# A chunk state summed in PSUM, and a square moved to ScalarE, in a hybrid RWKV-7 / RG-LRU / attention kernel

## The chip, the cores and the metric

The kernel runs on one core of a Trainium2 chip. The metric is the device time of one execution in microseconds. A core has five engines, each with its own in-order queue: TensorE (PE, with weight loads shown as PEld), VectorE (DVE), ScalarE (ACT), GpSimd (POOL) and SyncE (SP), which here issues the DMAs. SBUF is the working memory; PSUM is where TensorE writes its results, and VectorE and ScalarE read and write it too.

## The reference

Two layers over 512 tokens of width 1024. Each layer normalizes, projects to one wide vector, and runs three mixers side by side on slices of it: an RWKV-7 recurrence (8 heads of 64x64 state), an RG-LRU recurrence over 512 channels, and latent attention. Cut to what the change touches:

```python
def step(S, inp):                                  # RWKV-7, one token
    r_t, w_t, k_t, v_t, kk_t, b_t = inp
    sa = jnp.einsum('bhij,bhj->bhi', S, kk_t)
    S = S * w_t[:, :, None, :] - sa[..., None] * b_t[:, :, None, :] + v_t[..., None] * k_t[:, :, None, :]
    return S, jnp.einsum('bhij,bhj->bhi', S, r_t)
...
log_a = -LRU_C * gate_r * jax.nn.softplus(-lam)    # RG-LRU
a = jnp.exp(log_a)
bx = jnp.sqrt(-jnp.expm1(2.0 * log_a)) * (gate_i * xc)
_, h = lax.associative_scan(combine, (a, bx), axis=1)      # h_t = a_t h_(t-1) + bx_t
```

## The kernel before

All products with large weights are done as three float32r matmuls (L233, L234, L235): each operand is split into a rounded high part (ScalarE, L141) and the rest (GpSimd or VectorE, L229 and L211), and high x high, low x high and high x low are summed in PSUM. These projection matmuls are the bulk of TensorE's work, and the program threads them between the small matmuls of the recurrences.

The RWKV-7 recurrence runs in eight chunks of 64 tokens. `chunk(ch)` (L841) does one. If it is not the first, eight pairs of 64x64 matmuls with the state S (L849) correct the values, and two VectorE additions write them to UV (L852). Eight pairs with UV (L859) give the chunk's contribution `so`, in PSUM. The new state is (so + S) x pc, with pc the decay at the chunk's end, one number for each column: L863 adds, L864 multiplies; the first chunk has only a product (L866). The next chunk's L849 needs that state. Every second chunk also makes the outputs of the pair: matmuls with S (L877) and with UV (L883) into two PSUM tiles, a VectorE copy (L885) and a ScalarE square (L886) of each, and a reduction (L887). The small products of the chunks use `ck()`, which hands out two PSUM banks in turn.

The RG-LRU runs on four groups of 128 channels, in two pairs: `lru_b(0, 1)` and `lru_b(2, 3)`. For each group ScalarE makes a = exp(...) (helper line L138, after a table load, L136); GpSimd squares it (L702); VectorE makes (a^2 + 1) x th (L704) and a lower bound (L705); after another table load ScalarE takes the root (L138); GpSimd multiplies it into bx (L710); VectorE scans (L712; its opcode prints as SCALAR_TENSOR_TENSOR in the lists below); ScalarE squares the result (L716, L718), GpSimd sums the squares (L719), and VectorE applies gain and gate (L720). The convolution in front of the gates is three VectorE instructions (L681), and the gate matmuls behind it are L687. L691 is a GpSimd product of that part.

The order of this work comes from strings of step names. The stage of the change is the head of this one (H is `chunk`, B is `lru_b`, A the front half of the RG-LRU, f and t steps of projections):

```python
ORD3 = "B0 H0 H1 A2 H2 H3 A3 H4 H5 H6 H7 B1 N0 g0 g1 t0 t6 t1 ..."
```

Within that, a list scheduler orders the instructions of each engine by its own costs, so that an edited instruction can move its neighbours. Weights come through rings of buffers: three raw tiles (wr), four high (wH) and four low parts (wL).

Of the kernel before, what the change touches and what calls it, by code (L numbers as in the profile page):

```python
# [11 lines left out]
AF = mybir.ActivationFunctionType  # L12
ALU = mybir.AluOpType
# [34 lines left out]
def body(ctx, tc, x, wc, wl, wo, w2a2, gagx, wuq, wukv, vec, ln_g, fin_g, cst, out, depth=DEPTH):  # L48
    nc = tc.nc
    V, A, G = nc.vector, nc.scalar, nc.gpsimd  # L50
# [21 lines left out]
    def g2(shape=(128, 512)):  # L72
        return tl("g2", shape, F32, bufs=11)
# [59 lines left out]
    def act(out, in_, func, **kw):  # L133
        st = {AF.Sigmoid: "S", AF.Tanh: "S", AF.Sqrt: "Q"}.get(func, "E")
        if cur[0] != st:
            chained(A.preload_act_table_set(SETS[st]))  # L136
            cur[0] = st
        chained(A.activation(out=out, in_=in_, func=func, **kw))  # L138
# [182 lines left out]
    def one_layer(l):  # L321
# [375 lines left out]
        def lru_b(*js):  # L697
            for j in js:
                a, bx, th = st[j]
                act(a, a, AF.Exp, scale=nsp8[:, l, j:j + 1])  # L700
                a2 = g2()
                G.tensor_tensor(out=a2, in0=a, in1=a, op=ALU.mult)  # L702

                V.scalar_tensor_tensor(out=a2, in0=a2, scalar=1.0, in1=th, op0=ALU.add, op1=ALU.mult)  # L704
                V.tensor_scalar(out=a2, in0=a2, scalar1=1.0e-34, scalar2=None, op0=ALU.max)  # L705
                st[j] += (a2,)
            for j in js:
                a, bx, th, a2 = st[j]
# [130 lines left out]
        S = [None] * 8  # L839

        def chunk(ch):  # L841
# [11 lines left out]
            if ch < 7:  # L853
                so = ck([128, 4, 64])
                for p in range(4):
                    for e in range(2):
                        hr = slice(64 * e, 64 * e + 64)
                        hc = slice(e * 64, (e + 1) * 64)
                        PE.matmul(so[hr, p, :], BT[p][:, ch, hc], UV[:, p, ch, hc], start=True, stop=True)  # L859
                sn = S[ch + 1] = tl("S", [128, 4, 64], bufs=3)  # L860
                pc = PC[:, :, ch:ch + 1].to_broadcast([128, 4, 64])
                if ch:
                    V.tensor_tensor(out=sn, in0=so, in1=S[ch], op=ALU.add)  # L863
                    V.tensor_tensor(out=sn, in0=sn, in1=pc, op=ALU.mult)  # L864
                else:
                    V.tensor_tensor(out=sn, in0=so, in1=pc, op=ALU.mult)  # L866
            if par == 0:
                return
            yt = c2([128, 4, 2, 64])
# [357 lines left out]
```

## Time and profile before

| | us |
|---|---|
| three runs | 848.09, 848.45, 851.1 |
| median | 848.45 |
| profiled execution | 847.71 |
| its span | 845.9 |
| TensorE busy | 791.7 (94%) |
| VectorE busy | 538.9 (64%) |
| ScalarE busy | 519.3 (61%) |
| GpSimd busy | 353.3 (42%) |

The profile is of one execution. A row of the timeline gives the start in us from the span's start, the duration, the engine, the line, the operation with output and inputs by name, the count where neighbours are merged, and in brackets how long the engine stood idle before it and which engine's instruction ended that. A row that groups instructions gives their summed and mean durations, or in another view the least, median and greatest in ns. The windows give each engine's busy time in a stretch and the granted TensorE clock, where 1.00 is full rate. Durations of neighbours on one engine overlap a little, since the next one starts while the last one drains. A matmul's end is modelled.

### The profile page before, as it was taken

The numbers are of one execution on the slowest core, as the hardware profiler recorded it, in microseconds if no ns is written. First come the engines' busy times: TensorE is split into PE (matmuls) and PEld (weight loads), VectorE is DVE, ScalarE is ACT, GpSimd is POOL, SyncE is SP. The second block draws the span as 40 slices with busy tenths as digits, with TensorE's granted clock in tenths as the row PEclk, the third lists the DMA queues.
The fourth block names the chain that finished last, engine by engine and source line by source line (L and its number), as shares of the span: only waits on it lengthen the run. The fifth ranks groups of instructions, "written<-read, shape, count | busy, mean of one in ns | idle before, by whom it ended". The sixth has DMA issues, their size and how long they took to land. (4 is left out here: it accounts for less than half of the span.)

```text
span 845.9 us, 15219 instructions
## 1 busy us (share of the span) xinstructions
PE 791.7 (94%) x5696; PEld 619.4 (73%) x5696; DVE 538.9 (64%) x1115; ACT 519.3 (61%) x1018; POOL 353.3 (42%) x321
## 2 busy tenths in 40 slices
PE   4999999999879999999989999999998799999995
PEld 3878888886659877657778788888765697775674
DVE  5678776924977364774474966695367953577636
ACT  5667875657563576664467687845666436765635
POOL 0455557522452455022344556574143425530323
PEclk9999999999998999999999999999999899999998
DMA  7222134311113375123732233332001234731354
GB/s 246 98 76 74 66 111 132 112 58 33 33 39 113 120 229 193 55 90 92 272 122 89 75 100 100 101 112 92 30 26 43 80 95 140 244 120 50 112 174 162
DMA packets 49754, 91.07 MB, mean 108 GB/s; under 512 B 5520, under 2 KB 8336, under 8 KB 49680
## 3 DMA queue, kind: packets, MB, share of 16 engines
q1 hardware_dynamic: 49104, 89.05, 32.8%
q8 instruction: 45, 0.74, 0.4%
q10 hardware_dynamic: 576, 1.05, 0.3%
q14 instruction: 29, 0.24, 0.1%
HBM read 73.30 MB, written 16.78 MB: 106 GB/s over the span
## 5 line engine op out<-in xcount | busy, mean ns | idle before, releaser
L229 POOL TENSOR_TENSOR wL<-wr,wH 128x512 fp32r<-128x512 f32 (+1 forms) x148 | 196.8, 1336 | 283.9 <-ACT wH L141 270.4
L141 ACT ACTIVATE wH<-wr 128x512 fp32r<-128x512 f32 (+1 forms) x192 | 118.8, 622 | 142.8 <-PE acc L234 73.9
L233 PE MATMUL acc<-xH,wH 128*128 128x512 f32 (+1 forms) x496 | 191.9, 388 | 0.0
L234 PE MATMUL acc<-xL,wH 128*128 128x512 f32 (+1 forms) x496 | 189.3, 382 | 0.7 <-DVE xL L306 0.6
L235 PE MATMUL acc<-xH,wL 128*128 128x512 f32 (+1 forms) x496 | 188.5, 380 | 0.0
L234 PEld LDWEIGHTS acc<-xL,wH 128*128 128x128 f32 x496 | 94.0, 190 | 17.5 <-DVE xL L306 1.4
L233 PEld LDWEIGHTS acc<-xH,wH 128*128 128x128 f32 x496 | 93.5, 189 | 18.1 <-ACT xH L141 0.7
L235 PEld LDWEIGHTS acc<-xH,wL 128*128 128x128 f32 x496 | 93.9, 189 | 17.2
L233 PE MATMUL acc<-wH,c 128*128 128x512 f32 x192 | 82.5, 430 | 0.1
L234 PE MATMUL acc<-wL,c 128*128 128x512 f32 x192 | 76.7, 399 | 0.0
L235 PE MATMUL acc<-wH,c 128*128 128x512 f32 x192 | 76.2, 397 | 0.0
L141 ACT ACTIVATE UV<-ps 64x512 f32<-64x512 f32 (+4 forms) x112 | 52.4, 494 | 28.8 <-PE ps L1076 22.0
L229 DVE TENSOR_TENSOR wL<-wr,wH 128x512 fp32r<-128x512 f32 (+1 forms) x44 | 32.6, 744 | 53.0 <-ACT wH L141 52.9
L138 ACT ACTIVATE c<-acc,sm 128x128 f32<-128x128 f32 (+3 forms) x64 | 33.6, 528 | 19.0 <-DVE sm L1060 19.0
L1058 PE MATMUL acc<-am,am 128*128 128x128 f32 (+3 forms) x128 | 42.8, 447 | 0.9 <-ACT c L138 0.8
L234 PEld LDWEIGHTS acc<-wL,c 128*128 128x128 f32 x192 | 36.5, 190 | 8.7 <-issue 1.9
L233 PEld LDWEIGHTS acc<-wH,c 128*128 128x128 f32 x192 | 36.3, 189 | 8.7 <-issue 2.2
L235 PEld LDWEIGHTS acc<-wH,c 128*128 128x128 f32 x192 | 36.3, 189 | 8.2 <-issue 0.5
L136 ACT ACT_TABLE_LOAD x31 | 39.8, 1283 | 1.3 <-PEq L1215 0.7
L138 ACT ACTIVATE g<-g 128x512 f32<-128x512 f32 (+1 forms) x58 | 36.4, 628 | 4.6 <-DVE g L705 2.6
L369 POOL TENSOR_TENSOR g<-g,g 128x512 f32<-128x512 f32 x24 | 32.2, 1340 | 13.9 <-ACT g L138 13.9
L141 ACT ACTIVATE c<-g 128x512 fp32r<-128x512 f32 (+1 forms) x40 | 24.9, 629 | 18.8 <-DVE g L980 7.2
(219 smaller groups left out, 1587.7 us busy)
## 6 DMA issues: line engine op xcount, KB each, us to landing
wr<-in_wc_dram SPq DMA_DIRECT2D x116, 256.0 KB, 2.7
wr<-in_wo_dram SPq DMA_DIRECT2D x48, 256.0 KB, 3.4
hp<-dr SPq DMA_DIRECT2D x38, 256.0 KB, 3.5
dr<-hp SPq DMA_DIRECT2D x28, 256.0 KB, 3.3
dr<-g SPq DMA_DIRECT2D x16, 256.0 KB, 2.5
g<-dr SPq DMA_DIRECT2D x16, 256.0 KB, 3.5
wr<-in_wl_dram SPq DMA_DIRECT2D x16, 208.0 KB, 2.5
dr<-c SPq DMA_DIRECT2D x12, 256.0 KB, 3.7
```

The source lines that it names most:

```text
L136: chained(A.preload_act_table_set(SETS[st]))
L138: chained(A.activation(out=out, in_=in_, func=func, **kw))
L141: i = A.activation(out=out, in_=in_, func=AF.Copy, **kw)
L229: (V if wn[0] % wmod[0] == 0 or wn[0] <= 4 else G).tensor_tensor(out=L, in0=raw, in1=f(H), op=ALU.subtract)
L233: PE.matmul(o, a[0], b[0], start=start, stop=False)
L234: PE.matmul(o, a[0], b[1], start=False, stop=False)
L235: PE.matmul(o, a[1], b[0], start=False, stop=stop)
L369: G.tensor_tensor(out=z, in0=z, in1=s, op=ALU.mult)
L1058: PE.matmul(o[:, 0:n], qT[:, hd, qt * 128:n], K2[:, p, e, 0:n], start=True, stop=True)
```

## The change

The sum of the chunk's contribution and the old state is written back over the contribution, in PSUM, and the product with the decay reads it from there and writes the new state to SBUF. The first chunk's product is now the same line. In the RG-LRU the square of a is made by ScalarE instead of GpSimd, outside the helper that tracks activation tables; the counts of table loads are the same in both programs.

```diff
--- before.py
+++ after.py
@@ -699,7 +699,7 @@
                 a, bx, th = st[j]
                 act(a, a, AF.Exp, scale=nsp8[:, l, j:j + 1])
                 a2 = g2()
-                G.tensor_tensor(out=a2, in0=a, in1=a, op=ALU.mult)
+                A.activation(out=a2, in_=a, func=AF.Square)
 
                 V.scalar_tensor_tensor(out=a2, in0=a2, scalar=1.0, in1=th, op0=ALU.add, op1=ALU.mult)
                 V.tensor_scalar(out=a2, in0=a2, scalar1=1.0e-34, scalar2=None, op0=ALU.max)
@@ -860,10 +860,9 @@
                 sn = S[ch + 1] = tl("S", [128, 4, 64], bufs=3)
                 pc = PC[:, :, ch:ch + 1].to_broadcast([128, 4, 64])
                 if ch:
-                    V.tensor_tensor(out=sn, in0=so, in1=S[ch], op=ALU.add)
-                    V.tensor_tensor(out=sn, in0=sn, in1=pc, op=ALU.mult)
-                else:
-                    V.tensor_tensor(out=sn, in0=so, in1=pc, op=ALU.mult)
+
+                    V.tensor_tensor(out=so, in0=so, in1=S[ch], op=ALU.add)
+                V.tensor_tensor(out=sn, in0=so, in1=pc, op=ALU.mult)
             if par == 0:
                 return
             yt = c2([128, 4, 2, 64])
```

The same numbers of instructions are issued but for eight that pass from GpSimd to ScalarE. Each engine's list also comes out in another order, in the same way in both layers; elsewhere the lists differ in line numbers alone, but for one weight load on SyncE's queue in each layer that now stands ahead of three other loads. Lines behind the edit have numbers smaller by one (the additions of the sum print as L864, the product as L865, copy and square of the outputs as L884 and L885, the reduction as L886).

VectorE in layer 0, around chunk 5, whose state is S_2539; S_2518 is the state before it, UV the corrected values, g_455 and g_456 the squares of the second RG-LRU pair. Before:

```order
L704 SCALAR_TENSOR_TENSOR g_455_2657<-g_455_2657,g_423_2357 128x512
L852 TENSOR_TENSOR UV_319<-ck,UV_319 64x4x64 x2
L705 TENSOR_SCALAR g_455_2657<-g_455_2657 128x512
L704 SCALAR_TENSOR_TENSOR g_456_2662<-g_456_2662,g_443_2498 128x512
L863 TENSOR_TENSOR S_2539<-ck,S_2518 128x256
L885 COPY c_446_2542<-ps_2544 128x4x64
L864 TENSOR_TENSOR S_2539<-S_2539,PC_320 128x256
L885 COPY c_446_2542<-ps_2545 128x4x64
L705 TENSOR_SCALAR g_456_2662<-g_456_2662 128x512
```

and now:

```order
L852 TENSOR_TENSOR UV_319<-ck,UV_319 64x4x64 x2
L704 SCALAR_TENSOR_TENSOR g_455_2657<-g_455_2657,g_423_2357 128x512
L704 SCALAR_TENSOR_TENSOR g_456_2662<-g_456_2662,g_443_2498 128x512
L864 TENSOR_TENSOR ck<-ck,S_2518 128x256
L884 COPY c_446_2542<-ps_2544 128x4x64
L865 TENSOR_TENSOR S_2539<-ck,PC_320 128x256
L884 COPY c_446_2542<-ps_2545 128x4x64
L705 TENSOR_SCALAR g_455_2657<-g_455_2657 128x512
```

The two L852 stand ahead of both L704, and the bound L705 of the first square has moved from before the sum to behind the two copies.

ScalarE over the same time (g_420 and g_440 are a, wH parts of weights, ps_2544 and ps_2545 the outputs of chunks 4 and 5). Before:

```order
L138 ACTIVATE g_440_2490<-g_440_2490,nsp_103 128x512
L136 ACT_TABLE_LOAD
L141 ACTIVATE g_466_2734<-acc_2697 128x512
L141 ACTIVATE wH_2808<-wr_2806 128x416
L138 ACTIVATE g_455_2657<-g_455_2657 128x512
L886 ACTIVATE c_447_2543<-ps_2544 128x4x64
L886 ACTIVATE c_447_2543<-ps_2545 128x4x64
L138 ACTIVATE g_456_2662<-g_456_2662 128x512
L136 ACT_TABLE_LOAD
L141 ACTIVATE wH_2826<-wr_2824 128x416
```

and now:

```order
L138 ACTIVATE g_440_2490<-g_440_2490,nsp_103 128x512
L702 ACTIVATE g_455_2657<-g_420_2348 128x512
L702 ACTIVATE g_456_2662<-g_440_2490 128x512
L136 ACT_TABLE_LOAD
L141 ACTIVATE g_466_2734<-acc_2697 128x512
L141 ACTIVATE wH_2808<-wr_2806 128x416
L885 ACTIVATE c_447_2543<-ps_2544 128x4x64
L885 ACTIVATE c_447_2543<-ps_2545 128x4x64
L138 ACTIVATE g_455_2657<-g_455_2657 128x512
L141 ACTIVATE wH_2826<-wr_2824 128x416
L138 ACTIVATE g_456_2662<-g_456_2662 128x512
```

The squares of a stand ahead of the table load, and the first root (L138 on g_455) stands behind the two output squares instead of in front of them.

VectorE around chunk 6, whose new state S_2601 is the one that chunk 7 reads. Before:

```order
L712 SCALAR_TENSOR_TENSOR g_423_2357<-g_420_2348,g_422_2354 128x512
L712 SCALAR_TENSOR_TENSOR g_443_2498<-g_440_2490,g_442_2495 128x512
L863 TENSOR_TENSOR S_2601<-ck,S_2539 128x256
L229 TENSOR_TENSOR wL_2809<-wr_2806,wH_2808 128x416
L864 TENSOR_TENSOR S_2601<-S_2601,PC_320 128x256
L720 SCALAR_TENSOR_TENSOR g_423_2357<-g_423_2357,vecs,g_352_1723 128x512
L720 SCALAR_TENSOR_TENSOR g_443_2498<-g_443_2498,vecs,g_367_1818 128x512
L852 TENSOR_TENSOR UV_319<-ck,UV_319 64x4x64 x2
```

and now:

```order
L712 SCALAR_TENSOR_TENSOR g_423_2357<-g_420_2348,g_422_2354 128x512
L229 TENSOR_TENSOR wL_2809<-wr_2806,wH_2808 128x416
L864 TENSOR_TENSOR ck<-ck,S_2539 128x256
L712 SCALAR_TENSOR_TENSOR g_443_2498<-g_440_2490,g_442_2495 128x512
L865 TENSOR_TENSOR S_2601<-ck,PC_320 128x256
L720 SCALAR_TENSOR_TENSOR g_423_2357<-g_423_2357,vecs,g_352_1723 128x512
L720 SCALAR_TENSOR_TENSOR g_443_2498<-g_443_2498,vecs,g_367_1818 128x512
L852 TENSOR_TENSOR UV_319<-ck,UV_319 64x4x64 x2
```

The split L229 and the sum stand between the two scans, and only the product stands behind both.

TensorE at the end of the chunks. Before, behind chunk 7's last output matmuls and ahead of the first matmul of the next step (acc_2782):

```order
L883 MATMUL ps_2617<-UV_319,am_317 64x64
L883 MATMUL ps_2617<-UV_319,am_318 64x64
L233 MATMUL acc_2740<-xH_104,wH_2761 128x512
L234 MATMUL acc_2740<-xL_105,wH_2761 128x512
L235 MATMUL acc_2740<-xH_104,wL_2762 128x512
L233 MATMUL acc_2782<-wH_2790,xH_104 128x416
```

now, the last ones ahead of chunk 7's first matmul with the state (behind its outputs acc_2782 follows at once):

```order
L234 MATMUL acc_2740<-xL_105,wH_2761 128x512
L235 MATMUL acc_2740<-xH_104,wL_2762 128x512
L233 MATMUL acc_2740<-xH_104,wH_2761 128x512
L234 MATMUL acc_2740<-xL_105,wH_2761 128x512
L235 MATMUL acc_2740<-xH_104,wL_2762 128x512
L849 MATMUL ck<-S_2601,c_109_513 64x64 x2
```

The last three projection matmuls on acc_2740 have moved from behind chunk 7 to in front of it; all along the chunks one to three such matmuls have moved forward past a chunk's small ones.

## The prediction

> **What bounds the kernel now.** Line numbers are those of the kernel before. I read the page's first rows, then TensorE's timeline where the changed lines run, then the other engines around each wait found there.
>
> ```profile
> span 845.9 us, 15219 instructions
> PE 791.7 (94%) x5696; PEld 619.4 (73%) x5696; DVE 538.9 (64%) x1115; ACT 519.3 (61%) x1018; POOL 353.3 (42%) x321
> ```
>
> TensorE is idle for 845.9 - 791.7 = 54 us. The changed lines run in layer 0 between 207 and 257 us and again 413.5 us later. These are the waits above 1 us on TensorE there, four a layer (start, duration, instructions; in brackets the idle time and what ended it):
>
> ```profile
> 215.84 0.68 PE L849 MATMUL ck<-S,c 64*64 64x64 f32 x16 [1.24 <-DVE S L864]
> 224.31 1.93 PE L687 MATMUL ps<-g,w 64*64 64x512 f32 x8 [2.10 <-DVE g L681]
> 241.86 0.57 PE L883 MATMUL ps<-UV,am 128*64 128x64 f32 x12 [1.60 <-DVE UV L852]
> 253.56 0.80 PE L849 MATMUL ck<-S,c 64*64 64x64 f32 x10 [3.13 <-DVE S L864]
> ...
> 629.33 0.68 PE L849 MATMUL ck<-S,c 64*64 64x64 f32 x16 [1.25 <-DVE S L864]
> 637.82 2.78 PE L687 MATMUL ps<-g,w 64*64 64x512 f32 x8 [2.14 <-DVE g L681]
> 656.21 0.57 PE L883 MATMUL ps<-UV,am 128*64 128x64 f32 x12 [1.60 <-DVE UV L852]
> 667.90 0.51 PE L849 MATMUL ck<-S,c 64*64 64x64 f32 x10 [3.11 <-DVE S L864]
> ```
>
> They sum to 8.07 and 8.10 us: two waits for the chunk state S, one for the convolution of the RG-LRU (L681), one for the corrected values UV. So VectorE's queue bounds this stage, not TensorE. The windows of 8 us (stretch, its length, busy time of PE, PEld, DVE, ACT and POOL, granted clock, DMA) show two things more:
>
> ```profile
> 224.00:232.00 8.00, 7.39 (x124) 5.09 (x125) 7.68 (x15) 3.70 (x6) 1.60 (x1) 1.00 0.30 83
> 248.00:256.00 8.00, 4.81 (x63) 3.71 (x59) 7.97 (x8) 2.46 (x5) 6.51 (x4) 0.82 0.43 133
> 256.00:264.00 8.00, 7.76 (x56) 7.33 (x57) 6.33 (x13) 3.46 (x7) 2.44 (x2) 0.76 0.25 82
> 272.00:280.00 8.00, 8.00 (x46) 7.75 (x45) 3.69 (x22) 4.38 (x8) 2.59 (x2) 1.00 0.42 140
> ...
> 637.00:645.00 8.00, 7.18 (x80) 4.22 (x81) 6.93 (x13) 3.70 (x6) 1.44 (x3) 0.79 0.33 83
> 669.00:677.00 8.00, 6.73 (x47) 6.08 (x47) 6.39 (x13) 3.58 (x7) 1.23 (x1) 0.57 0.42 135
> ```
>
> Behind the stage TensorE has no gap (8.00 of 8.00 us at 272), so what it gains here should reach the end. And the clock falls after three of these waits, not after the 2.10 us one. Read as spells at half rate (0.18 + 0.24 missing over 8 us make 8 x 0.42 / 0.5 = 6.7 us, 0.21 make 3.4, 0.43 make 6.9), that is 17 us.
>
> **The change: prices.** The product on the state, the sum, the form that the new product takes (L866), an in-place sum in PSUM of nearly the same size (L739), and the square:
>
> ```profile
> L864 DVE TENSOR_TENSOR S<-S,PC x12: 412/613/1478, 215.4 to 666.4; 128x256 f32<-128x256 f32 x12
> L864 DVE TENSOR_TENSOR S<-S,PC 128x256 f32<-128x256 f32 x12 | 9.4, 787 | 0.1
> L863 DVE TENSOR_TENSOR S<-ck,S 128x256 f32<-128x256 f32 x12 | 5.1, 422 | 4.7 <-PE ck L859 4.4 <-PE ps L883 0.2
> L866 DVE TENSOR_TENSOR S<-ck,PC 128x256 f32<-128x256 f32 x2 | 0.8, 424 | 2.1 <-PE ck L859 2.1
> L739 DVE TENSOR_TENSOR ck<-ck,xt 128x240 f32<-128x240 f32 x4 | 1.7, 416 | 0.1
> L702 POOL TENSOR_TENSOR g<-g x8: 1040/1042/2015, 208.3 to 654.2; 128x512 f32<-128x512 f32 x8
> ```
>
> The product of two SBUF operands took 412 ns at best and 787 in the mean; the long ones run beside GpSimd. With one operand in PSUM the forms stay at 422 and 424. The in-place sum in PSUM is bounded by 416 (240 elements) from below and, from the nearest larger PSUM form, 424 from above; I take 424. So twelve pairs cost 12 x (0.424 + 0.424) instead of 12 x (0.422 + 0.787): VectorE saves 12 x 0.361 = 4.3 us, of which only what stands ahead of a TensorE wait counts. PSUM's bank is held one instruction longer, which costs nothing: its next writer, the next chunk's L849, needs the product anyway.
>
> [...]
>
> The eight squares leave GpSimd (1.04 us each, 2.0 when blocked) and cost ScalarE some 0.63 us each, as its root over a tile of that size does (below): 5.0 us. ScalarE is under half busy in the windows above, but its queue is in order, so what stands behind a square comes later.
>
> **Where this meets the path, layer 0.** Chunk 1 first (VectorE, then ScalarE's first root):
>
> ```profile
> 212.66 1.23 DVE L712 TENSOR_TENSOR_SCAN g<-g,g 128x512 f32<-128x512 f32 x1 [0.21 <-POOL g L710]
> 214.76 0.69 DVE L704 SCALAR_TENSOR_TENSOR g<-g,g 128x512 f32<-128x512 f32 x1 [0.87 <-POOL g L676]
> 215.37 0.42 DVE L864 TENSOR_TENSOR S<-S,PC 128x256 f32<-128x256 f32 x1
> ...
> 210.65 0.63 ACT L138 ACTIVATE g<-g 128x512 f32<-128x512 f32 x1
> ```
>
> L864 stands behind an L704 that idled 0.87 us: the row names a memset, but that stands right behind the second square on GpSimd, the operand that L704 reads. Now the first square delays table load, first root and scan by at most its 0.63: the scan runs from 213.3 to 214.5, L704 follows without a wait (the second square stands two rows behind the root, done by 213), the product ends at 215.5 instead of 215.79. **(a): 0.3 us earlier.** Two projection matmuls are also moved ahead of this L849.
>
> (b) From there to L687 VectorE is never idle. It begins 0.3 earlier, and one L852 is moved ahead of the last L681, one L885 away: **0.2 to 0.3 us earlier**, and the wait stays at 2.1 to 2.3 since TensorE comes sooner too.
>
> (c) Chunk 5. The pair of L852 stood behind an L704 that waited for both squares:
>
> ```profile
> 239.97 1.51 DVE L704 SCALAR_TENSOR_TENSOR g<-g,g 128x512 f32<-128x512 f32 x1 [1.47 <-POOL g L702]
> 243.66 1.11 DVE L864 TENSOR_TENSOR S<-S,PC 128x256 f32<-128x256 f32 x1
> ...
> 238.85 0.51 PE L849 MATMUL ck<-S,c 64*64 64x64 f32 x10
> ```
>
> In the new order both L852 come first and need only TensorE's L849, which starts at 238.85, or 0.7 sooner with (a), (b) and the two matmuls. So **the 1.60 us wait shrinks to about 0.4**. The product of chunk 5, before done at 244.77, then follows the pair of L852, two L704, the sum and a copy: near 241.8.
>
> (d) Chunk 7, the largest wait. Roots, products, VectorE's queue, and TensorE's work behind the chunk:
>
> ```profile
> 242.50 0.63 ACT L138 ACTIVATE g<-g 128x512 f32<-128x512 f32 x1 [0.80 <-DVE g L705]
> ...
> 246.25 1.30 POOL L710 TENSOR_TENSOR g<-g,g 128x512 f32<-128x512 f32 x1 [1.76 <-ACT g L138]
> 248.05 1.47 POOL L229 TENSOR_TENSOR wL<-wr,wH 128x416 fp32r<-128x416 f32 x1 [0.50 <-ACT wH L141]
> ...
> 247.16 3.44 DVE L712 TENSOR_TENSOR_SCAN g<-g,g 128x512 f32<-128x512 f32 x2
> 252.03 1.48 DVE L864 TENSOR_TENSOR S<-S,PC 128x256 f32<-128x256 f32 x1
> 253.43 2.42 DVE L720 SCALAR_TENSOR_TENSOR g<-g,vecs,g 128x512 f32<-128x512 f32 x2
> 255.78 0.74 DVE L852 TENSOR_TENSOR UV<-ck,UV 64x256 f32<-64x256 f32 x2
> ...
> 258.13 0.80 PE L233 MATMUL acc<-xH,wH 128*128 128x512 f32 x1
> 259.58 0.50 PE L233 MATMUL acc<-wH,xH 128*128 128x416 f32 x1
> ```
>
> The first root now stands behind two L886 squares and ends at 243.4 (before 243.13); its GpSimd product ends at 244.75. The second root waits for an L705 that this product blocks, and ends at 245.75. From here VectorE and GpSimd alternate. If each scan has to wait out one GpSimd operation (two scans took 3.44 where the one of chunk 1 took 1.23), the first ends at 247.2, the split L229 at 248.9, the sum at 249.3, the second scan at 251.2, the product at 251.55; if none waits, 250.5. Before, 253.51. I take the late end: **2.0 us earlier**. Behind it the two L720 take as long as before, so L852 comes at 254.0 (before 255.78) and TensorE's chunk block 1.8 earlier. The three projection matmuls that stood behind that block (258.13 to 259.58, 1.45 us at half clock) are moved ahead into the wait. So the next step, the first 128x416 matmul, starts 1.8 + 1.45 = **3.2 us earlier**; (a) to (c) are contained in it. A layer's bounds: 1.45 (only the filling) and 2.8 + 1.45 = 4.2 (no scan waits).
>
> Layer 1 has the same waits within 0.04 us: 2 x 3.2 = 6.4. The profiled execution took 847.71 us around a span of 845.9; the median of the runs is 848.45, 0.7 above it. So 841.3 for a profiled one and **842.0** for the median.
>
> **Rivals.** (1) The stage gains but half is given back: scans and L720 wait for GpSimd more often, or the roots come later. The late L720 (2.42 for two) speaks for it, the freed 2.0 us squares against. Bounds 1.45 to 2.2 us a layer: 844 to 846, take 845.
>
> (2) The clock no longer falls. After 1.60 and 2.10 us in layer 0 it stayed at 1.00, after 2.14 in layer 1 it fell. If the wait of chunk 7 shrinks enough, its block runs at full clock: 16 of L883's matmuls took 0.75 at full clock, 30 about 1.97 at half:
>
> ```profile
> 231.62 0.75 PE L883 MATMUL ps<-UV,am 128*64 128x64 f32 x16
> 256.24 1.97 PE L883 MATMUL ps<-UV,am 128*64 128x64 f32 x30 [0.30 <-DVE UV L852]
> ```
>
> At 1.2 for 30 that is 0.8, and as much (an estimate) in the part of the block ahead of them: 842.0 - 2 x 1.6 = 838.8; with layer 1's fall at L687 gone too (its 8 matmuls took 2.78, in layer 0 1.93) 838. [...]
>
> (3) Slower: the clock falls more. L687's wait grows to as much as 2.3, so layer 0 may fall there too, as layer 1 did at 2.14. If it fell at all four and held twice as long, 2 x (17 + 3.4) = 41 us instead of 17 would run at half rate: 24 x 0.5 = 12 lost against 6.4 gained, 854. It decides from 13 us more at half clock; against it, every spell seen ended within 7 us.
>
> (4) It does not do what it says, or the gain is absorbed later: 848.5. Against it, TensorE has no gap to absorb it in for tens of microseconds behind the stage.
>
> **Numbers.** Forecast 0.52, (1) 0.22, (2) 0.12, (3) 0.05, (4) 0.09. A measurement here can tell about 0.5% (4.2 us) from no change, so faster means below 844.2. Forecast and (2) are faster; a tenth of (1) lies below that bound and a twentieth of the forecast above it. Faster 0.63, same 0.32, slower 0.05. Range 837.5 to 847: from (2), with the early end of (d) in both layers, to the last of (1).
>
> **What would show it.** Right: sum and product both flat near 424 ns; no L704 waiting for a square; the 1.60 us wait under 0.6; L849 of chunk 7 near 251.6 and the first 128x416 matmul near 256.4, and the same 413.5 us on. Wrong: a sum in PSUM well above 424 ns; roots later than 244 and 246; scans above 2 us each; more than three stretches of half clock; or the stage 3 us shorter and the span not.

## The result, and the profile after

| | before | after |
|---|---|---|
| median of five runs, us | 848.58 (848.09 to 851.1) | 843.7 (842.16 to 845.5) |
| profiled execution, us | 847.71 | 842.16 |
| its span, us | 845.9 | 840.4 |

The ratio of after to before is 0.993, with a 95% interval of 0.9914 to 0.9945: 0.7% faster (the two medians alone give 0.994), where 842.0 us had been forecast. Four rows of the timeline above 1 us in a layer carried the prediction. These are TensorE's waits of after in the same place (start, duration, count; in brackets the wait), and the first 128x416 matmul behind them:

```profile
224.33 1.93 PE L687 MATMUL ps<-g,w 64*64 64x512 f32 x8 [2.40 <-DVE g L681]
240.21 0.69 PE L859 MATMUL ck<-UV,c 128*64 128x64 f32 x16 [0.38 <-DVE UV L852]
251.91 0.51 PE L849 MATMUL ck<-S,c 64*64 64x64 f32 x10 [3.16 <-DVE S L865]
254.57 1.97 PE L882 MATMUL ps<-UV,am 128*64 128x64 f32 x30 [1.26 <-DVE UV L852]
256.47 0.72 PE L233 MATMUL acc<-wH,xH 128*128 128x416 f32 x1
...
636.69 1.93 PE L687 MATMUL ps<-g,w 64*64 64x512 f32 x8 [2.39 <-DVE g L681]
652.54 0.69 PE L859 MATMUL ck<-UV,c 128*64 128x64 f32 x16 [0.38 <-DVE UV L852]
664.25 0.80 PE L849 MATMUL ck<-S,c 64*64 64x64 f32 x10 [3.20 <-DVE S L865]
666.92 1.97 PE L882 MATMUL ps<-UV,am 128*64 128x64 f32 x30 [0.30 <-DVE UV L852]
```

Chunk 1's wait of 1.24 is gone in both layers and chunk 5's of 1.60 is 0.38. The wait for the convolution (L687) grew to 2.40, and chunk 7's stayed at 3.16 to 3.20, since TensorE comes to it earlier as well. Behind it TensorE waits for L852 (the rows of L882): 1.26 us in layer 0, 0.30 in layer 1. VectorE's queue from chunk 5 to chunk 7:

```profile
241.95 0.40 DVE L865 TENSOR_TENSOR S<-ck,PC 128x256 f32<-128x256 f32 x1
...
245.55 1.22 DVE L712 TENSOR_TENSOR_SCAN g<-g,g 128x512 f32<-128x512 f32 x1
246.69 1.41 DVE L229 TENSOR_TENSOR wL<-wr,wH 128x416 fp32r<-128x416 f32 x1
248.13 0.43 DVE L864 TENSOR_TENSOR ck<-ck,S 128x256 f32<-128x256 f32 x1
249.27 2.27 DVE L712 TENSOR_TENSOR_SCAN g<-g,g 128x512 f32<-128x512 f32 x1 [0.71 <-POOL g L710]
251.46 0.39 DVE L865 TENSOR_TENSOR S<-ck,PC 128x256 f32<-128x256 f32 x1
251.77 2.42 DVE L720 SCALAR_TENSOR_TENSOR g<-g,vecs,g 128x512 f32<-128x512 f32 x2
254.12 0.74 DVE L852 TENSOR_TENSOR UV<-ck,UV 64x256 f32<-64x256 f32 x2
```

Read it from the bottom. L852 frees chunk 7's second half; ahead of it stand two L720, which nothing near needs. The product L865 frees chunk 7's first half. Its sum was done at 248.56, and 0.39 us of work would have given the state; but the second scan stands between, and waits 0.71 for GpSimd and runs 2.27. So 2.9 of the 3.16 us are a matter of order, not of price. The clock, in windows of 4 us of after (the third number from the right is the granted clock):

```profile
252.00:256.00 4.00, 2.74 (x74) 2.53 (x76) 4.00 (x6) 3.20 (x7) 3.66 (x3) 0.70 0.00 0
256.00:260.00 4.00, 4.00 (x20) 3.74 (x17) 3.83 (x10) 0.77 (x2) 0.90 (x1) 0.50 0.75 234
260.00:264.00 4.00, 4.00 (x21) 3.97 (x21) 3.73 (x11) 1.10 (x2) 1.08 (x1) 0.95 0.32 100
```

What is missing to 1.00 is 1.2 + 2.0 + 0.2 = 3.4 us. In the same way the stage from chunk 0's product to the token sums (L379) is measured in all kernels below. All times are us; "to 128x416" is from chunk 0's product on the state to the first 128x416 matmul, "to the sums" from that same product to the first L379, and the missing clock is (1 - granted clock) x 4 us, summed. Each cell has layer 0 and layer 1, of the one profiled execution; the ratios are of all executions.

| kernel | ratio to before (95%) | to 128x416 | to the sums | missing clock |
|---|---|---|---|---|
| before | 1 | 51.51, 52.37 | 69.74, 71.42 | 3.4, 5.1 |
| the change | 0.993 (0.9914 to 0.9945) | 48.15, 48.17 | 68.12, 66.74 | 3.4, 3.4 |
| sum in PSUM alone | 0.998 (0.9966 to 0.9995) | 50.74, 52.27 | 69.97, 71.19 | 3.4, 5.1 |
| square alone | 0.9892 (0.9874 to 0.991) | 48.15, 48.33 | 66.43, 66.25 | 1.7, 1.7 |
| before, order of chunk 5 | 0.9961 (0.9944 to 0.9977) | 50.21, 52.49 | 68.29, 71.12 | 3.4, 5.1 |
| change, one L720 later | 0.9907 (0.9879 to 0.9935) | 47.73, 47.91 | 66.13, 65.99 | 1.7, 1.7 |
| change, work behind the wait | 0.9958 (0.9935 to 0.9981) | 51.86, 48.96 | 70.06, 67.15 | 3.4, 0 |
| change, work inside the wait | 0.9885 (0.987 to 0.99) | 46.80, 48.32 | 64.98, 66.50 | 0, 1.7 |
| change, late scan | 0.9794 (0.9775 to 0.9814) | 43.81, 43.83 | 61.83, 61.98 | 0, 0 |
| square alone, late scan | 0.9831 (0.9801 to 0.9862) | 43.83, 43.83 | 63.42, 63.41 | 0, 0 |
| both, late scan, one L720 later | 0.9832 (0.9803 to 0.9861) | 43.28, 43.31 | 63.20, 63.31 | 0, 0 |
| the same, wrong split moved | 0.9862 (0.9845 to 0.9878) | 43.27, 43.30 | 64.10, 65.65 | 0, 1.7 |
| the same, right split moved | 0.978 (0.9767 to 0.9794) | 43.30, 43.31 | 61.48, 61.36 | 0, 0 |

From before to the change the stage got 141.16 - 134.86 = 6.3 us shorter in the profiled executions, and the span 5.5: the work ahead of the stage, between the layers and behind it took 0.8 more. But the gain was not spread as forecast. At the first 128x416 matmul layer 0 was 3.4 us ahead and layer 1 4.2; at the token sums they were 1.6 and 4.7 ahead.

### The profile page after: what moved, and what is told of

The parts are those of the page before. It is cut to its first block, busy times and chain, and to the rows that moved or that the text cites. A ratio compares the mean times of both kernels' runs of the same rounds, so it can differ in the third digit from the quotient of the medians.

```text
span 840.4 us, 15211 instructions
## 1 busy us (share of the span) xinstructions
PE 789.6 (94%) x5696; PEld 618.5 (74%) x5696; DVE 533.2 (63%) x1115; ACT 522.6 (62%) x1026; POOL 344.4 (41%) x313
## 5 line engine op out<-in xcount | busy, mean ns | idle before, releaser
L229 POOL TENSOR_TENSOR wL<-wr,wH 128x512 fp32r<-128x512 f32 (+1 forms) x148 | 198.2, 1345 | 283.7 <-ACT wH L141 278.9
L229 DVE TENSOR_TENSOR wL<-wr,wH 128x512 fp32r<-128x512 f32 (+1 forms) x44 | 35.1, 801 | 51.1 <-ACT wH L141 51.0
L138 ACT ACTIVATE c<-acc,sm 128x128 f32<-128x128 f32 (+3 forms) x64 | 33.6, 528 | 19.0 <-DVE sm L1059 18.7
L138 ACT ACTIVATE g<-g 128x512 f32<-128x512 f32 (+1 forms) x58 | 36.4, 627 | 2.2 <-DVE g L499 0.9
L141 ACT ACTIVATE c<-g 128x512 fp32r<-128x512 f32 (+1 forms) x40 | 24.7, 628 | 13.5 <-DVE g L979 7.2
```

Of the source, the lines that this page charges most:

```text
L141: i = A.activation(out=out, in_=in_, func=AF.Copy, **kw)
L229: (V if wn[0] % wmod[0] == 0 or wn[0] <= 4 else G).tensor_tensor(out=L, in0=raw, in1=f(H), op=ALU.subtract)
```

## Experiments

In kernels with an order given the line numbers are somewhat higher; operation and tiles name the instruction. An order is given by a dependency without a semaphore, which only tells the scheduler what to issue first.

### The two parts alone

The sum alone: the square goes back to GpSimd.

```diff
-                A.activation(out=a2, in_=a, func=AF.Square)
+                G.tensor_tensor(out=a2, in0=a, in1=a, op=ALU.mult)
```

> The sum in PSUM alone; the squares stay on GpSimd. VectorE's order stays that of before: in chunk 5 the pair of L852 stands behind an L704, both scans and L229 stand ahead of the product on the state of chunk 6. Theory Order (what counts is the place of the L852 of chunk 5 and of the product of chunk 6 in VectorE's queue, the price of an instruction counts only right ahead of a TensorE wait): the 1.60 us wait stays within 0.2; the product of chunk 6 shrinks from 1.48 to 0.42 us, so TensorE starts chunk 7 about 1.1 us earlier than before (252.5) and a layer gains 0.7 to 1.1 us: 846.6 (846 to 847.3). Theory Price (the 4.3 us that VectorE saves with the shorter product make most of the gain): 844 to 845, with the 1.60 us wait shrunk too.

0.998. VectorE around chunk 6, in the kernel with the sum alone:

```profile
253.28 0.41 DVE L865 TENSOR_TENSOR S<-ck,PC 128x256 f32<-128x256 f32 x1
253.62 3.09 DVE L720 SCALAR_TENSOR_TENSOR g<-g,vecs,g 128x512 f32<-128x512 f32 x2
256.63 0.74 DVE L852 TENSOR_TENSOR UV<-ck,UV 64x256 f32<-64x256 f32 x2
```

The product shrank from 1.48 to 0.41 us as priced, and chunk 7's wait from 3.13 to 2.05. But the two L720 behind it grew from 2.42 to 3.09, beside a GpSimd product that runs from 254.44 to 256.16. At the first 128x416 matmul layer 0 gained 0.77 us and layer 1 0.10. VectorE's busy time over the span, from which the prediction took 4.3 us, went from 538.9 to 538.7. The wait of chunk 5 stayed, at 1.54. Theory Order gave 846 to 847.3 (0.997 to 0.9985), theory Price 844 to 845: by the time and by chunk 5's wait Order holds, but layer 1 gained 0.10 us where it expected 0.7 to 1.1.

The square alone: the kernel before with the one line on ScalarE.

> The squares on ScalarE alone; sum and product as before. VectorE's order changes as with the whole change in chunk 5 (both L852 ahead of the L704), and in chunk 6 the product on the state comes even ahead of the second scan; but seven projection matmuls instead of none now stand behind chunk 7 on TensorE. Theory Order: the 1.60 us wait is under 0.6; the product of chunk 6 ends near 249.4 to 250.1 (in the changed kernel 251.85), chunk 7 starts 1.4 to 2.1 us earlier than there, but its second half waits for L852 behind the second scan and one L720 until about 254.3, and the seven matmuls follow (1.7 us at full, 3.3 at half clock): first 128x416 matmul near 257.5 to 259, a gain of 0.6 to 2 us a layer, 844.5 to 847.4. Theory Price: without the shorter product at least half of the gain is gone, 846 to 848.5, and the product of chunk 6 takes over 1 us and holds chunk 7 up. The two parts alone should not add up to the whole by Order (they lead to three different orders), and should by Price.

0.9892: not only most of the gain, but more than the whole change. The product on the state, from SBUF as before, in the square's kernel, and below it the product from PSUM in the changed kernel (least, median, greatest in ns):

```profile
L864 DVE TENSOR_TENSOR S<-S,PC x12: 406/414/425, 215.1 to 658.3; 128x256 f32<-128x256 f32 x12
```

```profile
L865 DVE TENSOR_TENSOR S<-ck,PC x14: 392/418/425, 208.3 to 663.8; 128x256 f32<-128x256 f32 x14
L702 ACT ACTIVATE g<-g x8: 613/618/633, 208.8 to 651.9; 128x512 f32<-128x512 f32 x8
```

Before it had been 412/613/1478. With the squares off GpSimd and the order that follows, the product costs 414 ns from SBUF and 418 from PSUM. So the two parts remove the same 0.36 us; with the square moved the sum in PSUM saves nothing.

Theory Price's first half is refuted (the product takes over 1 us nowhere). Order named the place right and its price wrong: chunk 7 did start earlier (product done at 248.11, expected 249.4 to 250.1), but the time is 0.9892 x 848.58 = 839.4, and 844.5 to 847.4 was expected. The reason stands in the last two columns of the table. At the first 128x416 matmul this kernel is no further than the whole change (48.15 and 48.33 against 48.15 and 48.17); behind it, it misses 1.7 us of clock in each layer and the whole change 3.4. Over the five executions of each, the mean granted clock is 0.990 against 0.985, which is 8.2 us of missing clock in 839.1 against 12.6 in 841.8.

### Why the whole is slower than one of its parts

VectorE ahead of L687, in the changed kernel and then with the square alone:

```profile
221.06 1.45 DVE L720 SCALAR_TENSOR_TENSOR g<-g,vecs,g 128x512 f32<-128x512 f32 x1
222.44 1.75 DVE L681 SCALAR_TENSOR_TENSOR g<-g,vecs,g 128x512 f32<-128x512 f32 x1
```

```profile
221.09 1.44 DVE L681 SCALAR_TENSOR_TENSOR g<-g,vecs,g 128x512 f32<-128x512 f32 x1
222.45 1.75 DVE L720 SCALAR_TENSOR_TENSOR g<-g,vecs,g 128x512 f32<-128x512 f32 x1
```

L687 needs the L681. In the changed kernel the scheduler puts an L720 ahead of it, as in the kernel before, and TensorE waits 2.40 us; with the square alone 1.36. Two more differences stand behind it: in chunk 6 of the square alone the product comes ahead of the second scan, and on TensorE seven projection matmuls stay behind chunk 7, where the changed kernel has none. One order given to the changed kernel undoes the first of these. The L720 of group 1 becomes a step of its own, E1, behind tap[2], the last L681 of group 2:

```diff
+        def gated(j):
+            i = V.scalar_tensor_tensor(out=yb[j], in0=yb[j], scalar=vc("out_g", j), in1=gz[j], op0=ALU.mult, op1=ALU.mult)
+            after(i, tap[2])
...
-    ORD3 = "B0 H0 H1 A2 H2 H3 A3 H4 H5 H6 H7 B1 N0 g0 g1 t0 t6 t1 t2 t4 t5 t3 t7 T0 R0 Y0 g2 g3 T1"
+    ORD3 = "B0 H0 H1 A2 E1 H2 H3 A3 H4 H5 H6 H7 B1 N0 g0 g1 t0 t6 t1 t2 t4 t5 t3 t7 T0 R0 Y0 g2 g3 T1"
```

> The changed kernel, with one order given: the second L720 of the first pair stands behind the last L681 of the third on VectorE. With that the rest of VectorE's order falls out as with the square alone (the product of chunk 6 ahead of the second scan), and six projection matmuls stand behind chunk 7. Theory Order: the time is that of the square alone, 0.989 (0.987 to 0.991) of before; L687 waits 1.4 us instead of 2.40, chunk 7 under 1 us instead of 3.16. Rival Bank or Price (the sum in PSUM itself makes the whole change slower than the square alone, by holding its bank or by its own time): it stays at 0.992 to 0.995.

The waits came out as expected: L687 1.39, chunk 7's first half 0.16 (instead of 3.16), with a second wait of 3.00 for L852. The second change of order followed by itself, as the scheduler then also put the product ahead of the scan; six projection matmuls stand behind chunk 7. The missing clock is 1.7 in each layer as with the square alone. By the time alone it is not settled: 0.9907, with an interval that holds both 0.989 and 0.992. By the rows, the sum in PSUM is not what makes the whole slower; the order that it brings is.

### The order of chunk 5 alone

The kernel before, with the L704 of the second pair (i below) behind chunk 5's last L852 (uadd[5]).

```diff
+                if j > 1:
+                    tc.add_manual_dep(getattr(i, "ins", i), getattr(uadd[5], "ins", uadd[5]).name, NOSYNC, reason="behind chunk 5")
```

> The kernel before, with one order given: the L704 of the second pair stand behind chunk 5's L852 on VectorE. Squares and sums untouched. Theory Order: the 1.60 us wait shrinks under 0.6 with nothing else changed. That gain is kept inside the stage, since chunk 7 then waits longer: the first root is not earlier (its L705 comes later), six projection matmuls now stand behind chunk 7, and L852 of chunk 7 still stands behind both scans and one L720. So the whole is 846.5 to 849. Theory Price or a theory of the squares: the wait shrinks only with the square off GpSimd, so it stays over 1.2 us here, 848.5.

TensorE in layer 0 of that kernel:

```profile
241.52 0.69 PE L863 MATMUL ck<-UV,c 128*64 128x64 f32 x16 [0.38 <-DVE UV L856]
...
251.24 0.51 PE L853 MATMUL ck<-S,c 64*64 64x64 f32 x10 [1.83 <-DVE S L868]
255.44 1.97 PE L887 MATMUL ps<-UV,am 128*64 128x64 f32 x30 [2.21 <-DVE UV L856]
```

The 1.60 us wait is 0.38 with nothing but the order changed, so step (c) was right that it hung on the place of the L852 in the queue, and it does not hang on the squares' engine. The gain did not last: chunk 7 then waits 1.83 + 2.21 instead of 3.13 + 0.30, and at the first 128x416 matmul 1.3 us are left in layer 0 and none in layer 1. 0.9961 x 848.58 is 845.3; 846.5 to 849 was expected, so 1 us less than that.

### What the half clock costs

The changed kernel, with 24 matmuls of 128x256 more in each layer, placed on TensorE ahead of chunk 7. They read xH and write where nothing reads, so the computation has 48 matmuls more and is otherwise the same. In both tries below one L229 and the splits of the second pair's outputs are also kept behind chunk 7's L852, to hold VectorE's order.

```diff
+            for i in range(n):
+                d = PE.matmul(cks[:, ckn[0] % 2, 256:512], xH[:, 0, 0:128], xH[:, 0, 0:256], start=True, stop=True)
...
+                        if ch == 7:
+                            tc.add_manual_dep(getattr(i, "ins", i), getattr(dummies[0], "ins", dummies[0]).name, NOSYNC, reason="behind the dummies")
```

> The changed kernel, with 24 extra 128x256 matmuls a layer on TensorE in the wait ahead of chunk 7 (they write a part of a PSUM bank that nothing reads, so the result is the same). They take some 2.8 us, so the wait for S shrinks from 3.16 to under 0.5 us while nothing that the kernel needs comes earlier. Theory Order: the fall of the clock behind chunk 7 follows from the long wait, and is part of the price of that wait: chunk 7's block and the first 128x416 matmuls now run at full clock, a layer gains 1.7 to 3.3 us between chunk 7 and the token sums, 837 to 840.5 (0.986 to 0.991 of before). Rival: the clock falls there for another reason (the small matmuls, or a fixed time), and the extra matmuls only use the wait: 843 to 844.5, granted clock behind chunk 7 still under 0.9.

0.9958, or 845.0 us: outside of both expectations, since the edit did not fill the wait. The extra matmuls, in layer 0 and then in layer 1:

```profile
254.74 4.52 PE L852 MATMUL ck<-xH 128*128 128x256 f32 x24 [3.17 <-DVE S L883]
667.03 3.14 PE L852 MATMUL ck<-xH 128*128 128x256 f32 x24 [3.17 <-DVE S L883]
```

They themselves waited for the product on the state (they write a tile whose other part the product reads), so they stand behind the wait and add 3 us or more to the path. The same wait of 3.17 us, with the same matmuls behind it, was followed by half clock in layer 0 and by full clock in layer 1. So here neither the wait's length nor what follows it decides. What differs is where the wait lies: in this trace the granted clock changes only at whole multiples of 3.413 us from its other changes, and these are the stretches of that grid about the two waits (TensorE's busy time is the second number behind the stretch, the granted clock the third from the right):

```profile
252.57:255.98 3.41, 1.25 (x10) 1.25 (x11) 3.41 (x4) 1.58 (x4) 1.52 (x2) 1.00 0.63 196
255.98:259.39 3.41, 3.41 (x20) 3.19 (x21) 1.06 (x1) 2.05 (x5) 3.41 (x3) 0.50 0.00 0
...
662.17:665.58 3.41, 1.70 (x8) 1.06 (x6) 2.67 (x3) 1.20 (x2) 3.41 (x3) 1.00 0.48 143
665.58:668.99 3.41, 1.96 (x16) 1.96 (x17) 3.41 (x4) 2.29 (x5) 1.52 (x3) 1.00 0.38 136
668.99:672.40 3.41, 3.41 (x89) 3.14 (x88) 1.92 (x5) 1.34 (x3) 2.74 (x2) 1.00 0.02 5
```

In layer 0 one stretch takes most of the wait, TensorE is busy for 1.25 of its 3.41 us, and the next stretch runs at 0.50. In layer 1 two stretches share the wait, TensorE is busy for 1.70 and 1.96 us of them, and the clock stays. The last section says how far this holds in the other traces.

The second try writes to a free tile, and stands between the last projection matmul and L849.

```diff
-                d = PE.matmul(cks[:, ckn[0] % 2, 256:512], xH[:, 0, 0:128], xH[:, 0, 0:256], start=True, stop=True)
+                o = ps()
+                dummies[0] = [PE.matmul(o[:, 0:256], xH[:, 0, 0:128], xH[:, 0, 0:256], start=True, stop=True) for i in range(n)]
```

> The changed kernel with the 24 extra 128x256 matmuls a layer once more, now into a PSUM tile that is free, so that they run inside the wait for S of chunk 7 and not behind it. Nothing that the kernel needs comes earlier: chunk 7's first matmul starts at 251.5 to 252, as in the changed kernel, its second half waits for L852 as before (1.26 us). Theory Clock (the 3.16 us wait costs its half-clock spell behind chunk 7 on top of itself, and in the changed kernel that is 3.4 us of lost clock a layer): the spell shrinks or goes, the first 128x416 matmul comes 0.8 to 1.5 us earlier, and the kernel takes 837 to 840.5 us (0.987 to 0.991 of before), as the square alone. Rival (the spell comes from the shorter wait or the small matmuls too): granted clock behind chunk 7 as in the changed kernel, 0.992 to 0.995.

0.9885. The wait filled, in layer 0:

```profile
248.98 3.03 PE L855 MATMUL ps<-xH 128*128 128x256 f32 x24
251.94 0.62 PE L870 MATMUL ck<-S,c 64*64 64x64 f32 x13
...
254.48 1.15 PE L907 MATMUL ps<-UV,am 128*64 128x64 f32 x30 [1.14 <-DVE UV L875]
255.56 0.46 PE L242 MATMUL acc<-wH,xH 128*128 128x416 f32 x1
```

Here the scheduler put the product ahead of the second scan, but L849 stands behind the extra matmuls anyway: chunk 7 starts at the same time as in the changed kernel (251.94 and 251.91) and its second half waits 1.14 (1.26), but the 30 matmuls behind that take 1.15 instead of 1.97 us, and the 128x416 ones run at full clock at once. No work of the kernel was saved; 3.4 us a layer of missing clock are gone behind chunk 7, and the time went from 0.993 to 0.9885. Theory Clock holds: where a spell follows the long wait, its price comes on top of the wait's. The number is that of the prediction's second rival (838 to 838.8): 0.9885 x 848.58 = 838.8. In layer 1 of the same execution the clock fell elsewhere, at L687, after 2.39 us:

```profile
633.15 3.45 PE L696 MATMUL ps<-g,w 64*64 64x512 f32 x8 [2.39 <-DVE g L690]
```

### The order that the profile asks for

The changed kernel, with the second scan of the second pair (the first i below) and both L720 (the second) behind chunk 7's last L852, uadd[7].

```diff
+                if j == 3:
+                    after(i, uadd[7])
...
+                if j > 1:
+                    after(i, uadd[7])
```

> The changed kernel, with one order given: the second scan of the second pair and both L720 stand behind chunk 7's L852 on VectorE; the program's work is the same. Theory Order: the product of chunk 6 follows its sum at once and ends near 249.0 (251.85 in the changed kernel); chunk 7 waits under 1.2 us instead of 3.16, its second half under 0.6, the clock stays at full, and the first 128x416 matmul, three projection matmuls later, starts at 252.3 to 253.5 instead of 256.47. A layer gains 3 to 4 us against the changed kernel: 835.5 to 838. Rival Absorbed (what lies behind the stage sets the time: the weights of the 128x416 matmuls, or the late scan and what it feeds): under 1.5 us in all, 842 to 844. Rival Clock (only the fall of the clock behind the long wait costs): 838 to 840, with the gain in the rows at half clock.

VectorE, then TensorE, then the window of 8 us with the granted clock, of that kernel:

```profile
248.33 0.43 DVE L873 TENSOR_TENSOR ck<-ck,S 128x256 f32<-128x256 f32 x1
248.79 0.42 DVE L874 TENSOR_TENSOR S<-ck,PC 128x256 f32<-128x256 f32 x1
250.00 0.75 DVE L861 TENSOR_TENSOR UV<-ck,UV 64x256 f32<-64x256 f32 x2 [0.78 <-PE ck L858]
251.34 1.21 DVE L717 TENSOR_TENSOR_SCAN g<-g,g 128x512 f32<-128x512 f32 x1
```

```profile
249.28 0.51 PE L858 MATMUL ck<-S,c 64*64 64x64 f32 x10 [1.01 <-DVE S L874]
252.36 0.35 PE L233 MATMUL acc<-wH,xH 128*128 128x416 f32 x1
```

```profile
248.00:256.00 8.00, 6.99 (x102) 6.28 (x101) 7.09 (x12) 5.01 (x11) 8.00 (x5) 1.00 0.57 184
```

The scan that took 2.27 takes 1.21 in its new place. Chunk 7 waits 1.01, its second half does not wait in the list of waits at all, and the first 128x416 matmul stands at 252.36 (252.3 to 253.5 expected, 256.47 in the changed kernel). 0.9794 x 848.58 = 831.1, and 835.5 to 838 was expected. Counted from chunk 0's product each layer gained 4.3 us up to the 128x416 matmuls, where 3 to 4 were expected; the spell of half clock behind them, which is gone too, had been left out: from there to the token sums it is 18.02 and 18.15 us, in the changed kernel 19.97 and 18.57.

### The price of the sum in PSUM, order held

The same late scan and L720, with the square alone; and then with both parts, with the L720 of the first pair behind its L681 as above. The two have the same VectorE order but for the sum, which has passed one L229, and a few rows behind chunk 7; TensorE has seven and six projection matmuls behind chunk 7.

> The squares on ScalarE, sum and product as before (SBUF), and the second scan of the second pair and both L720 given a place behind chunk 7's L852 on VectorE. Theory Order: both waits of the square alone stay short (L687's 1.4 us, chunk 7's 0.7), the 2.74 us wait for L852 of chunk 7 goes too: the first 128x416 matmul at 252 or earlier at full clock, 826 to 831 (0.973 to 0.979 of before). Theory Price: the product from SBUF takes over 0.6 us in the mean beside GpSimd and this kernel stays behind the next by 1.5 us or more.

> The changed kernel (sum in PSUM and squares on ScalarE) with the order of the kernel above on VectorE: the second L720 of the first pair behind the last L681 of the third, the second scan of the second pair and both L720 behind chunk 7's L852. The two kernels differ in the sum and the product on the state alone. Theory Order: the same time within 1.5 us (0.002), since the products of neither stand beside long GpSimd work any more. Theory Price: this one is 1.5 to 4 us faster. Rival Bank (a sum kept in PSUM holds the bank longer and delays the next chunk): this one is slower by over 1.5 us.

0.9831 and 0.9832 (means of 835.1 and 835.0 us in the same session): no difference clear of noise, so neither Price nor Bank. Up to the first 128x416 matmul the kernel with PSUM is 0.5 us ahead in each layer (chunk 7 waits 0.17 instead of 0.73, since the L229 no longer stands between its sum and its product). Both missed the time expected (0.973 to 0.979), and are slower than the kernel of the last section although up to the 128x416 matmuls they are as fast or faster. Here is why, in the kernel with both parts: a new wait, 13 us behind the first 128x416 matmul.

```profile
266.32 0.46 PE L234 MATMUL acc<-wL,xH 128*128 128x416 f32 x1 [1.52 <-DVE wL L229]
```

The low part of the sixth weight is split on VectorE behind the group norm's square root and its four products; in the kernel of the last section it stood ahead of the four products, at 261.97. So the next wait in line is one of the same kind.

### Two tries at that wait

The split on GpSimd, which in that kernel was busy for 1.38 us from 260 to 264 and not at all from 264 to 268.

```diff
+            wmod[0] = 1000 if kk in (3, 7) else WC
             W = weights(wl[l, :, kk, :], LAT)
```

> The kernel with both parts of the change and the late scan and L720, and beside that the split (L229) of the last two weights of the 128x416 matmuls on GpSimd instead of VectorE, where they stood behind the group norm and TensorE waited 1.52 us. Theory Order: the wait goes, TensorE has no gap from chunk 7 to the token sums, 1.3 to 1.6 us a layer earlier: 830.5 to 832.5 (0.977 to 0.980 of before). Rival (GpSimd's split takes over 1.1 us beside VectorE, or the next transfer of weights is late in its turn): the wait stays over 1 us, 0.982 to 0.984.

The weights come in the order 0, 6, 1, 2, 4, 5, 3, 7, and the sixth is number 5; number 3 was on GpSimd already. So the split that TensorE waits for stayed on VectorE, the group norm's four products ahead of it took 3.38 us beside GpSimd's extra split (2.50 before that), and the wait grew:

```profile
262.55 3.38 DVE L909 TENSOR_TENSOR c<-c,vr 128x512 f32<-128x512 f32 x4
265.86 0.58 DVE L229 TENSOR_TENSOR wL<-wr,wH 128x416 fp32r<-128x416 f32 x1
...
266.49 0.46 PE L234 MATMUL acc<-wL,xH 128*128 128x416 f32 x1 [2.42 <-DVE wL L229]
```

0.9862. The outcome is the rival's, over 0.984 even, but not for the rival's reason: the edit took the wrong weight. With `kk in (5, 7)` in its place:

> As the run before, but with the right weights: the split that TensorE waited for on VectorE is that of the sixth weight (2.42 us there, 1.52 with both on VectorE), and now the sixth and the eighth are split on GpSimd. Its first part of ScalarE is done near 260, so GpSimd's split is done near 261.5, ahead of TensorE's need near 264. Theory Order: no gap from chunk 7 to the token sums, 830 to 832.5 us (0.976 to 0.980 of before), as the kernel with the sum in PSUM and the late scan alone. Rival (the next thing in line, the group norm or a transfer, is late in its turn): 0.982 or above, with a new wait of over 1 us ahead of the token sums.

0.978 x 848.58 = 829.9. TensorE has no wait above 0.25 us between chunk 7 and the token sums, and the stage from chunk 7 on is full:

```profile
248.00:256.00 8.00, 8.00 (x108) 7.39 (x104) 7.42 (x11) 5.14 (x11) 8.00 (x5) 1.00 0.62 199
264.00:272.00 8.00, 8.00 (x46) 7.73 (x45) 6.79 (x29) 3.75 (x7) 2.60 (x2) 1.00 0.42 127
```

This kernel and that with the late scan added to the change alone (0.9794) beat both kernels of the case by more than 1%; between the two the intervals do not tell.

## Why the prediction was right, and where not

**What bounds the kernel** was right, and more so than the forecast used: the experiment that only gave VectorE another order took 11 us more out of the kernel (0.993 to 0.9794). The list of waits was short by one: in layer 1 of the kernel before, TensorE also waits 1.27 us for L852 at 670.57, where layer 0 has 0.30.

**The prices** of the instructions were right: 418 ns for the product, 5.1 us for the twelve sums (429 ns each, where 424 was taken), 618 for the square. The product from PSUM took 418 ns in the median (392 to 425, the changed kernel), the one from SBUF 414 (406 to 425, the square alone). What failed is the step "VectorE saves 12 x 0.361 = 4.3 us" as a gain of the sum in PSUM. The 0.36 us were time that the product lost beside GpSimd. With the square alone it is gone as well (414 ns), and with the sum alone it passed to the two L720. The prediction had the row that said so (412 at best, 787 in the mean) and took the mean as the price of the form. The rows also show where the two forms part. Beside the same GpSimd product (L691), chunk 2's product took 0.94 and 0.80 us in the two layers with both operands in SBUF (before), and 0.42 in both with one in PSUM (the change). Beside L719, chunk 6's in layer 0 took 1.48 before and 0.41 with the sum alone. In the four kernels where all 14 products of the PSUM form were read (the change, the sum alone, the change with one L720 later, both with late scan and one L720 later) the longest took 0.43. Why GpSimd's work spares that form was not shown.

**(a)** Product of chunk 1 0.3 us earlier: 215.79 before, 215.53 after, in an execution that began the stage 0.25 later: 0.3 by the profile's clock, 0.5 counted from chunk 0's product. Right, or somewhat better. **(b)** L687 0.2 to 0.3 earlier, counted from chunk 0's product: 16.24 before, 16.01 after. Right, with a wait of 2.40 where 2.1 to 2.3 was said. What it did not see is that an L720 stands ahead of the last L681; with the square alone that is the other way round, and L687 comes at 14.34. **(c)** 1.60 to 0.4: measured 0.38. Product of chunk 5 near 241.8: 242.35.

**(d)** ended where it was said, by a somewhat other way. Product of chunk 6: 251.55 said, 251.85 measured. L852: 254.0 and 254.12. First 128x416 matmul: 256.4 and 256.47. The second root was late,

```profile
244.98 0.55 ACT L141 ACTIVATE wH<-wr 128x416 fp32r<-128x416 f32 x1 [1.30 <-PE acc L234]
245.67 0.63 ACT L138 ACTIVATE g<-g 128x512 f32<-128x512 f32 x1
```

because a weight part for which ScalarE waits on TensorE's matmuls had moved in front of it: it ended at 246.30, where "roots later than 244 and 246" was to be a sign against the forecast. The first scan was shorter than said (1.22) and made up for it.

**The sum** of 6.4 us is the step that failed, though the stage got 6.3 shorter and the time is within the range: that it met the number so closely is luck. "The three projection matmuls (1.45 us at half clock) are moved ahead" counted them as gone. They are, but the half-clock spell is as long as it was: 3.4 us of missing clock in layer 0 before and after. It now lies on the 128x416 matmuls (0.55 each where 0.35 is full rate), so of the 3.4 us that layer 0 had gained at the first of them 1.6 are left at the token sums. Layer 1 makes up for that, and not by the change's doing: before, the clock fell after L687's wait of 2.14 us there; after it did not, at 2.39. That is 1.7 us of missing clock, and a kernel with the same stretch of order lost it again (the filled wait above, 2.39). So a term was too large in layer 0 and missing in layer 1. Over all executions on record the clock gives less than that, 0.9 us: 13.5 us of missing clock in the mean before (56 executions, (1 - granted clock) x span), 12.6 after (5). The range's ends do not follow from their working either: the second rival with the early end of (d) in both layers is 836 to 836.8 and not 837.5, and (1) ends at 846 and not 847.

**The rivals.** Nothing (848.5) and slower (854) are ruled out by the time; no more spells than before were seen. Half given back (844 to 846, taken as 845) is not ruled out by the time: the median of 843.7 is nearer to 845 than to 842.0, while the ratio gives 842.6 (841.3 to 843.9), nearer to the forecast. In layer 0 half the gain was in fact lost again, but to the clock and not, as this rival had it, to scans and roots. The second rival, the clock that no longer falls, was real, as a price: it did not come with this change, since chunk 7's wait did not shrink, and it is worth some 4 us when the wait is filled (0.993 to 0.9885). Its 1.2 us for 30 matmuls at full clock does not follow from 0.75 for 16 by proportion (that is 1.41), but was met (1.15). What the prediction did not work out is chunk 7's new wait: the state came 1.66 us earlier (253.51 and 251.85), TensorE 1.68 (250.43 and 248.75), so the wait stayed.

## What to carry to other kernels

Ask of a slow instruction whether its mean or its least duration is its price; where they differ (here 412 and 787 ns), look at what it runs beside: here the difference came from GpSimd's work, and the edit that shortened the instruction passed the loss to the next in the queue. When an edit sits in a list that a scheduler orders, read which independent work has come ahead of the instruction that the busiest engine waits for: here a scan and two products that nobody needed soon cost 11 us, and the form of the sum nothing. A wait is paid twice where the clock falls behind it: in the changed kernel chunk 7's 3.16 us were followed by 3.4 us of missing clock. Moving three matmuls from behind that wait to ahead of it only moved the spell to what came next (3.4 us missing in layer 0 before and after); with the wait at 1.01 us (the late scan) none was missing. Where the clock can fall, compare several executions before a gain of one or two us is put down to an edit.

## What the runs showed of the hardware

The missing clock comes in portions and on a grid. In each of the 13 traces the granted clock, from its first rise on, changes only at whole multiples of 3.413 us from its other changes, and in the stage it is down for one or two such stretches at a time. Down means 0.50, so one stretch is 1.7 us of missing clock, and the missing clock of a layer is 0, 1.7, 3.4 or 5.1 us.

Whether a spell comes is not told by the wait's length: after 2.38 to 2.40 us it came in one layer of two kernels and not in six other such places, and after 3.17 us it came in one layer and not in the other. TensorE's busy share in each stretch of the grid tells nearly all of it. In the 13 traces the clock fell 46 times, 45 of them behind a stretch with a share of 0.49 or less (the other 0.55). Of some 3000 stretches behind which it stayed at full rate, eight had 0.50 or less (0.43 to 0.50). It came back behind stretches of 0.88 and more, and stayed down behind 0.43 to 0.77 and once behind 0.90. So no stretch had to be idle as a whole, and waits under 3.4 us were enough: in the stage the clock fell in the kernel before behind shares of 0.23, 0.37 and 0.41 (the stretches from 249.65, 635.36 and 666.08, with waits of 3.13, 2.14 and 3.11), and in the changed kernel behind 0.41 and 0.38 (from 250.16 and 659.76, with 3.16 and 3.20). The bounds are rough, since the ends of matmuls are modelled.

This accounts for the two lengths of spell: in the changed kernel the stretch behind the fall at chunk 7 has a share of 0.71 and 0.69, with small matmuls and the wait for L852 in it, and a second one at half rate follows; with the square alone that stretch is full, and the spell is one stretch long. The grid begins at another place in each trace, and no run here could set it, so which waits it cuts in two is taken here for chance. The 12 executions of the kernel with the work behind the wait, which are of one program, have mean granted clocks between 0.987 and 0.997 and times between 840.88 and 848.86 us, the shorter ones in the main with the higher clock.
